# Wider rows for the modulation matrix, and an earlier silu, in a two-block kernel

## The chip, the cores and the metric

The kernel runs as one program on one core of one Trainium2 chip. The metric is the device time of one execution in microseconds (us); three executions of the kernel before took 1585.89, 1587.98 and 1588.04 us, and their median, 1587.98 us, is the time before. One more execution was recorded by the hardware profiler; it took 1586.62 us.

## The reference

Two transformer blocks follow each other on 256 tokens of width 1024, all in float32. The first block has a mixer (`w_in`, a short convolution and a gated recurrence), cross attention to 256 memory rows, and a mixture of 16 experts. The second block has two layers with three attention branches each; every layer takes its norms through a modulation that depends on a condition vector `c` (for the tokens) or `c_ctx` (for 256 context rows):

```python
for l in range(DEPTH_2):
    ...
    shift, scale, gate = jnp.split(jax.nn.silu(c) @ w_ada[l] + b_ada[l], 3, axis=-1)
    shift_c, scale_c, gate_c = jnp.split(jax.nn.silu(c_ctx) @ w_ada[l] + b_ada[l], 3, axis=-1)
    h = rms_norm_2(x, norm_g[l]) * (1.0 + scale[:, None]) + shift[:, None]
    hc = rms_norm_2(ctx, norm_g[l]) * (1.0 + scale_c) + shift_c
    ...
    x_new = x + gate[:, None] * merge_branches(o_na, o_mla, o_diff, z, gm, w_br[l], w_out[l])
```

`w_ada[l]` is 1024 x 3072, so 12 MB per layer are read to be multiplied by two vectors. None of this depends on the tokens: it can be computed at any time before the first norm of its layer.

## The kernel before, in words

**Order.** The kernel's instructions are written by a small planner inside the kernel file. Each part of the work is a generator ("fiber") with a priority and a clock of its own; `run` (L215) always takes the fiber that can start first by an estimate of each engine's time (`self.E`), and among equal ones that of the lowest priority number. `_pe` (L347) is its estimate for a matmul, `_later` (L248) moves a fiber's clock forward. The program is planned five times. Each pass fetches weights in the order in which the pass before used them, and the last pass repeats the order of the best of three. So a change of an estimate anywhere can move instructions everywhere.

**Weights.** All weights come in pieces ("units") of 512 KB, loaded by SyncE's queue in one fixed order (`_wdma`, L452), at most R units ahead (R is 5 at the start). A unit of most matrices is split by ScalarE and VectorE into two float32r parts, `wh` and `wl`, and used in three matmuls. A unit of `w_ada` is "plain": TensorE takes the float32 rows `w` as they landed.

**Modulation.** `ada(l)` (L1713) is a fiber of priority -6, ahead of everything. `silu_c` (L899) computes silu of both vectors and writes it 16 times over into `sil`, so that the stationary operand of a matmul has 32 columns. The four column groups of the array (32 columns each) then work on four pieces of `w_ada` at once and write four quarters of the partitions of one PSUM tile. A unit is two blocks of 128 rows by 512 columns of `w_ada` (runs of 2 KB in HBM); each block makes four matmuls of 128 moving columns, one for each column group. There are 24 units in a layer, in two PSUM tiles (4 and 2 column ranges of 512). When a tile is complete, ScalarE copies it out, TensorE transposes it, and VectorE adds the bias into `adacol`; from that `adaab` (the factors of the norm) is made.

Units of layer 1, and those of layer 0 but for the first `A0 = 2`, wait until the planner's TensorE clock is P1 = 4000 or P0 = 6000 ns further: they are strewn into the other work, one at a time.

**Start.** `setup` (L870) loads the tokens `X` on SyncE's queue, `cols` (all the short vectors, the two conditions among them) on ScalarE's, constants on GpSimd's. The fiber `tokens` starts at 5300 ns of the planner's clock (XT): a sum of squares on ScalarE and VectorE, a chain of tiny VectorE instructions for the inverse root, two scalings of X, 16 transposes on TensorE, the split of the transposed tokens into `hi` and `lo`, and the products with `w_in`. `silu_c` is started at 6800 ns by `context` (L2612): one ScalarE instruction and three of VectorE.

Of the kernel before, what the change touches and what calls it, by code (L numbers as in the profile page):

```python
# [14 lines left out]
OP = mybir.AluOpType  # L15
# [125 lines left out]
class Core:  # L141
# [14 lines left out]
    GPRIO, YPRIO = -1, 1.5  # L156
    MEMT, TOEP, CRIT = 40000, 20000, -4
    AH0, AH2 = 4, 1
    A0, P0, P1, AP0, AP1 = 2, 6000, 4000, -6, -6
    MFP = 0.5  # L160
    MEMP = 1
    GC, GW = 1, 7
# [1550 lines left out]
    def ada(self, l, *evs):  # L1713

        yield from self.wait(*evs)
        col = self.sb.tile([128, 24, 2], F32, name=f"adacol{l}", tag=f"adacol{l}", bufs=1)
        sil = self.sil.rearrange("p k r s -> p k (r s)")
        for g in ((0, 1, 2, 3), (4, 5)):
            ps = yield from self.palloc("pg")
            n = 128 * len(g)  # L1720
            for i, c in enumerate(g):
                for u in range(0, 8, 2):
                    if l or c * 4 + u // 2 >= self.A0:
                        self._later(self.E["pe"] + (self.P1 if l else self.P0))
                        yield
                    w = yield from self.wget("w_ada_2", (l,), u, u + 2, c * 512, c * 512 + 512, True)
                    for k in (u, u + 1):
                        for j in range(4):
                            self.mm(ps[32 * j:32 * j + 32, i * 128:i * 128 + 128], sil[:, k],
                                    w.raw[:, k - u, j * 128:j * 128 + 128], k == 0, k == 7, self.PAR[4])  # L1730
                        if k == u:
                            yield
                    self.wput(w)
                    yield
            r = yield from self.alloc("S", [128, 512])
            self.act(r[:, :n], ps[:, :n])
            self.free(ps)
            yield
            ps = yield from self.palloc("pa")
            for i in range(len(g)):  # L1740
                self.tr(ps[:, i * 128:i * 128 + 128], r[:, i * 128:i * 128 + 128])
            self.free(r)
            yield
            for i, c in enumerate(g):
                b = self.colv("b_ada", l * 24 + 4 * c, 4)
                pv = ps[:, i * 128:i * 128 + 128].rearrange("p (j r) -> p j r", j=4)
                self.tt(col[:, 4 * c:4 * c + 4], pv[:, :, 0:2], b[:, :, None].to_broadcast([128, 4, 2]), OP.add)
            self.free(ps)
            yield
        a = self.sb.tile([128, 2, 16], F32, name=f"adaab{l}", tag=f"adaab{l}", bufs=1)  # L1750
        for s in range(2):
            self.stt(a[:, s, 0:8], col[:, 8:16, s], 1.0, self.colv("norm_g", l * 8, 8), OP.add, OP.mult)
            self.cp(a[:, s, 8:16], col[:, 0:8, s])
        self.ada_ab[l], self.ada_g[l] = a, col
        self.set(self.ev_ada[l])
# [855 lines left out]

    def context(self):  # L2612
        norm = self.spawn(self.mem_norm(), prio=self.MEMP, t=self.MEMT)
        sil = self.spawn(self.silu_c(), prio=self.CRIT, t=6800.0, name="setup")
        self.ev_lb = self.spawn(self.lower(), prio=self.CRIT, t=self.LBT, name="setup")
        self.spawn(self.ada(0, sil), prio=self.AP0, name="ada")
        yield from self.mem_kv(norm)
        yield from self.ctx_hidden()
        yield from self.wait(self.ev_l0a)
        self.cur.prio = self.AP1  # L2620
        yield from self.ada(1)
# [114 lines left out]
```

## Time and profile before

| | before |
|---|---|
| median of 3 executions | 1587.98 us |
| their lowest and highest | 1585.89, 1588.04 us |
| profiled execution, its time | 1586.62 us |
| profiled execution, span from first to last instruction | 1584.8 us |
| TensorE busy | 1540.4 us, 97% |
| VectorE, ScalarE busy | 974.0 us, 749.4 us |
| moved by DMA | 305.15 MB, 48 loads of 512 KB of `w_ada` among them |

The span is what the views of the trace are measured in; the execution's own time has 1.8 us around it. PE is TensorE's matmuls, PEld its loading of stationary operands (which overlaps PE), DVE VectorE, ACT ScalarE, SP SyncE, whose queue issues the weight loads. A matmul of float32 on plain data shows as two records: the kernel has 384 of them in `ada`, the trace 768.

### The profile page before, as it was taken

Reading aid. Unit: us, or ns where it says so; the run is one execution under the profiler, and the core shown is the slowest. Engines: PE = TensorE matmul, PEld = TensorE weight load, DVE = VectorE, ACT = ScalarE, POOL = GpSimd, SP = SyncE. Lnnn points to the kernel's source line nnn. Section 1 sums busy time; section 2 is a strip of 40 time slices with the busy share of each in tenths; the row PEclk is TensorE's granted clock in tenths of the full one; section 3 lists DMA queues with packets and bytes.
Section 4 is the critical chain, followed back from the end, with each engine's and each line's share of the span. In section 5 each row is a group of like instructions: output and inputs, shape, how many; then the busy total and the mean of one; then the engine's idle time right before and its main releaser. Section 6 shows DMA issues by size and latency. Waiting matters only on the chain.

```text
span 1584.8 us, 25949 instructions
## 1 busy us (share of the span) xinstructions
PE 1540.4 (97%) x10202; PEld 1234.6 (78%) x10202; DVE 974.0 (61%) x1995; ACT 749.4 (47%) x1321; POOL 56.8 (4%) x91
## 2 busy tenths in 40 slices
PE   6999999999999999998999999999999999999898
PEld 6899897763554458886888777888888879989797
DVE  5877557722132257768765454754897766967755
ACT  5525345422322145747643345553464465645652
POOL 0000030000000001011000000000010200000000
PEclk9999999999999999999999999999999999999999
DMA  9766676589999996655324444443755425333341
GB/s 343 247 209 217 201 221 230 173 309 380 386 386 349 347 381 199 184 159 123 101 82 129 134 153 133 136 101 129 242 173 164 116 67 147 116 105 94 117 152 65
DMA packets 198939, 305.15 MB, mean 193 GB/s; under 512 B 10672, under 2 KB 97456, under 8 KB 198816
## 3 DMA queue, kind: packets, MB, share of 16 engines
q1 hardware_dynamic: 194384, 293.11, 56.3%
q0 software_dynamic: 3856, 9.64, 2.2%
q8 instruction: 81, 1.33, 0.3%
q10 hardware_dynamic: 576, 0.72, 0.2%
q14 instruction: 42, 0.34, 0.1%
HBM read 302.34 MB, written 2.90 MB: 193 GB/s over the span
## 4 chain that ended last, share of the span: by engine, by line
PE 60%; DVE 4%; ACT 1%; issue 1%; DVEq 0%; ACTq 0%
PE p L369 56%; PE p L374 4%; DVE t L392 1%; ACT t L382 1%; DVE wl L392 1%; DVE t L404 1%; DVE t L411 0%; ACT wh L382 0%; DVE t L413 0%; DVE X L392 0%; DVE p L392 0%; DVE t L397 0%; DVE t L399 0%; DVE t L406 0%; DVE t L420 0%
## 5 line engine op out<-in xcount | busy, mean ns | idle before, releaser
L369 PE MATMUL p<-t,wh 128*128 128x256 f32 (+1 forms) x2640 | 562.4, 309 | 0.0
L392 DVE TENSOR_TENSOR wl<-w,wh 128x1024 fp32r<-128x1024 f32 (+3 forms) x314 | 371.4, 1205 | 149.7 <-ACT wh L382 144.0
L369 PEld LDWEIGHTS p<-t,wh 128*128 128x128 f32 x2640 | 424.7, 190 | 32.5 <-issue 9.4
L369 PE MATMUL p<-wh,t 128*128 128x512 f32 (+1 forms) x1288 | 414.8, 394 | 2.3 <-DVE t L404 1.9
L369 PE MATMUL p<-t,wl 128*128 128x256 f32 (+1 forms) x1312 | 399.6, 305 | 2.2 <-DVE wl L392 2.2
L382 ACT ACTIVATE t<-p 128x512 f32<-128x512 f32 (+5 forms) x381 | 192.3, 528 | 411.3 <-PE p L369 316.8
L382 ACT ACTIVATE wh<-w 128x1024 fp32r<-128x1024 f32 (+3 forms) x314 | 316.8, 1042 | 58.5 <-PE p L369 23.4
L369 PEld LDWEIGHTS p<-wh,t 128*128 128x128 f32 x1288 | 242.8, 189 | 59.2 <-issue 6.8
L369 PEld LDWEIGHTS p<-t,wl 128*128 128x128 f32 x1312 | 249.8, 190 | 13.6 <-DVE wl L392 2.8
L369 PE MATMUL p<-wl,t 128*128 128x512 f32 (+1 forms) x644 | 251.1, 390 | 3.3 <-DVE wl L392 3.2
L369 PE MATMUL p<-t,t 128*64 128x128 f32 (+8 forms) x1824 | 222.4, 309 | 7.6 <-ACT t L382 6.2
L369 PEld LDWEIGHTS p<-t,t 128*64 128x64 f32 (+3 forms) x1824 | 177.3, 170 | 52.8 <-issue 24.9
L382 ACT ACTIVATE t<-p,t 128x512 f32<-128x512 f32 (+2 forms) x200 | 115.2, 597 | 126.6 <-PE p L369 84.0
L369 PE MATMUL p<-w,t 128*64 128x512 f32 x768 | 174.8, 598 | 0.0
L369 PEld LDWEIGHTS p<-wl,t 128*128 128x128 f32 x644 | 121.9, 189 | 27.1 <-DVE wl L392 5.1
L374 PE MATMUL p<-csts,t 128*128 128x128 f32 (+1 forms) x848 | 120.7, 278 | 12.8 <-ACT t L382 5.8
L369 PEld LDWEIGHTS p<-w,t 128*64 128x64 f32 x768 | 51.6, 136 | 95.6 <-issue 89.7
L374 PEld LDWEIGHTS p<-csts,t 128*128 128x128 f32 (+1 forms) x848 | 96.5, 140 | 34.5 <-ACT t L382 13.4
L392 DVE TENSOR_TENSOR t<-t,t 128x512 f32<-128x512 f32 (+9 forms) x226 | 106.4, 499 | 15.8 <-ACT t L382 13.0
L382 ACT ACTIVATE t<-p,cols 128x256 fp32r<-128x256 f32 (+4 forms) x91 | 51.3, 606 | 109.7 <-PE p L374 75.5
L411 DVE TENSOR_REDUCE t<-p 128x1 f32<-128x512 f32 (+1 forms) x124 | 84.7, 683 | 29.4 <-PE p L369 28.2
L404 DVE SCALAR_TENSOR_TENSOR t<-t,p 128x512 f32<-128x512 f32 x70 | 47.6, 683 | 78.7 <-PE p L369 39.8
(96 smaller groups left out, 694.0 us busy)
## 6 DMA issues: line engine op xcount, KB each, us to landing
w<-in_w_in_dram SPq DMA_DIRECT2D x206, 512.0 KB, 4.5
w<-in_w_gate_dram SPq DMA_DIRECT2D x64, 512.0 KB, 10.7
w<-in_w_up_dram SPq DMA_DIRECT2D x64, 512.0 KB, 10.6
w<-in_w_down_dram SPq DMA_DIRECT2D x64, 512.0 KB, 10.7
w<-in_w_ada_dram SPq DMA_DIRECT2D x48, 512.0 KB, 4.4
w<-in_w_out_dram SPq DMA_DIRECT2D x32, 512.0 KB, 4.3
w<-in_w_br_dram SPq DMA_DIRECT2D x28, 512.0 KB, 3.4
w<-in_w_kv_dram SPq DMA_DIRECT2D x16, 512.0 KB, 4.4
```

The lines of the kernel that those rows point to most:

```text
L369: self.nc.tensor.matmul(out, lhsT, rhs, start=start, stop=stop)
L374: self.nc.tensor.transpose(out, in_, self.ident[:k, :k])
L382: self.nc.scalar.activation(out, in_, func, bias=bias, scale=scale, **kw)
L392: self._e(eng, self._n(out), False, after).tensor_tensor(out, a, b, op=op)
L404: e.scalar_tensor_tensor(out, a, s, b, op0=op0, op1=op1)
L411: e.tensor_reduce(out, a, axis=AX, op=op, negate=True)
```

## The change

A unit of `w_ada` becomes one block of 128 rows by 1024 columns (runs of 4 KB), and each column group takes 256 of these columns in one matmul. A layer has three column ranges of 1024 instead of six of 512. For the first PSUM tile the two column ranges alternate inside the loop over the eight row blocks. The number of units, loads, bytes, copies out, transposes and bias additions stays; the number of matmuls is halved. The first *three* row blocks of the first column range are now free of the planner's spacing (A0 = 3); all units of the second and third range keep it. `silu_c` starts at 3500 ns of the planner's clock, ahead of the tokens' 5300.

```diff
-    A0, P0, P1, AP0, AP1 = 2, 6000, 4000, -6, -6
+    A0, P0, P1, AP0, AP1 = 3, 6000, 4000, -6, -6
...
-        for g in ((0, 1, 2, 3), (4, 5)):
+        for g in ((0, 1), (2,)):
             ps = yield from self.palloc("pg")
-            n = 128 * len(g)
-            for i, c in enumerate(g):
-                for u in range(0, 8, 2):
-                    if l or c * 4 + u // 2 >= self.A0:
+            n = 256 * len(g)
+            for k in range(8):
+                for i, c in enumerate(g):
+                    if l or c or k >= self.A0:
                         self._later(self.E["pe"] + (self.P1 if l else self.P0))
                         yield
-                    w = yield from self.wget("w_ada_2", (l,), u, u + 2, c * 512, c * 512 + 512, True)
-                    for k in (u, u + 1):
-                        for j in range(4):
-                            self.mm(ps[32 * j:32 * j + 32, i * 128:i * 128 + 128], sil[:, k],
-                                    w.raw[:, k - u, j * 128:j * 128 + 128], k == 0, k == 7, self.PAR[4])
-                        if k == u:
-                            yield
+                    w = yield from self.wget("w_ada_2", (l,), k, k + 1, c * 1024, c * 1024 + 1024, True)
+                    for j in range(4):
+                        self.mm(ps[32 * j:32 * j + 32, i * 256:i * 256 + 256], sil[:, k], w.raw[:, 0, j * 256:j * 256 + 256],
+                                k == 0 and i == 0, k == 7 and i == len(g) - 1, self.PAR[4])
                     self.wput(w)
                     yield
...
-            for i in range(len(g)):
+            for i in range(2 * len(g)):
                 self.tr(ps[:, i * 128:i * 128 + 128], r[:, i * 128:i * 128 + 128])
...
             for i, c in enumerate(g):
-                b = self.colv("b_ada", l * 24 + 4 * c, 4)
-                pv = ps[:, i * 128:i * 128 + 128].rearrange("p (j r) -> p j r", j=4)
-                self.tt(col[:, 4 * c:4 * c + 4], pv[:, :, 0:2], b[:, :, None].to_broadcast([128, 4, 2]), OP.add)
+                for h in range(2):
+                    b = self.colv("b_ada", l * 24 + 8 * c, 8)[:, h::2]
+                    m = 2 * i + h
+                    pv = ps[:, m * 128:m * 128 + 128].rearrange("p (j r) -> p j r", j=4)
+                    self.tt(col[:, 8 * c + h:8 * c + 8:2], pv[:, :, 0:2], b[:, :, None].to_broadcast([128, 4, 2]), OP.add)
...
-        sil = self.spawn(self.silu_c(), prio=self.CRIT, t=6800.0, name="setup")
+        sil = self.spawn(self.silu_c(), prio=self.CRIT, t=3500.0, name="setup")
```

## Rows read from the trace of the kernel before

**Rows 1.** The page: busy us (share of the span) and instructions by engine.
```profile
PE 1540.4 (97%) x10202; PEld 1234.6 (78%) x10202; DVE 974.0 (61%) x1995; ACT 749.4 (47%) x1321; POOL 56.8 (4%) x91
```

**Rows 2.** Windows, by stage: span, busy (instructions) of PE, PEld, DVE, ACT, POOL, clock, DMA.
```profile
60.00:205.00 145.00, 145.00 (x1179) 129.85 (x1178) 100.72 (x156) 57.52 (x77) 2.99 (x2) 1.00 0.62 206
...
870.00:1010.00 140.00, 139.02 (x1066) 109.64 (x1067) 77.74 (x217) 61.32 (x125) 0.00 (x0) 1.00 0.44 141
```

**Rows 3.** Waits of PE over the whole span: us in total, times, longest us.
```profile
PE p L369 <- DVE t L397: 11.1, 1, 11.1
...
PE p L374 <- DVE t L392: 4.2, 2, 3.2
...
PE p L369 <- DMA w<-in_w_ada_dram: 0.2, 1, 0.2
```

**Rows 4.** Timeline of PE around the unit at 23.32 us.
```profile
22.87 0.40 PE L369 MATMUL p<-t,wh 128*128 128x256 f32 x2
23.11 0.28 PE L369 MATMUL p<-t,wl 128*128 128x256 f32 x1
23.32 0.64 PE L369 MATMUL p<-w,sil 128*32 128x128 f32 x16
23.89 0.50 PE L369 MATMUL p<-t,wh 128*128 128x256 f32 x2
```

**Rows 5.** Windows inside that unit: span, PE busy (records begun), clock, DMA.
```profile
23.30:23.48 0.18, 0.16 (x8) 1.00 1.08 347
23.30:23.56 0.26, 0.24 (x8) 1.00 1.06 347
23.30:23.59 0.29, 0.27 (x12) 1.00 1.07 350
...
23.30:23.70 0.40, 0.38 (x16) 1.00 1.07 353
```

**Rows 6.** Window over plain matmuls of 512 columns, two column groups (64 wide).
```profile
328.30:335.70 7.40, 7.34 (x34) 1.00 0.52 179
```

**Rows 7.** Timeline of PE, start of the program.
```profile
11.11 1.08 PE L369 MATMUL p<-w,sil 128*32 128x128 f32 x16 [11.11 <-DVE t L397]
12.37 1.08 PE L369 MATMUL p<-w,sil 128*32 128x128 f32 x16 [0.17 <-DMA w<-in_w_ada_dram]
13.38 2.75 PE L374 MATMUL p<-csts,t 128*128 128x128 f32 x16
...
16.63 0.50 PE L369 MATMUL p<-t,wh 128*128 128x256 f32 x2
```

**Rows 8.** Timeline of ACT and DVE, start of the program.
```profile
6.25 1.06 ACT L382 ACTIVATE t<-X 128x1024 f32<-128x1024 f32 x1 [3.76 <-DMA X<-in_x_dram]
...
9.77 1.15 ACT L382 ACTIVATE t<-X,t 128x1024 f32<-128x1024 f32 x1 [2.26 <-DVE t L404]
13.85 1.06 ACT L382 ACTIVATE wh<-w 128x1024 fp32r<-128x1024 f32 x1 [2.93 <-DMA w<-in_w_in_dram]
...
10.07 0.29 DVE L416 COPY sil<-silc 128x256 f32<-128x256 f32 x1
10.28 0.75 DVE L397 TENSOR_SCALAR t<-X,t 128x1024 f32<-128x1024 f32 x1
```

**Rows 9.** DMA issues: the load of cols, KB and us from issue to landing.
```profile
cols<-in_cols_dram ACTq DMA_DIRECT2D x1, 80.5 KB, 3.4
```

**Rows 10.** Waits of PE in the first 60 us: us in total, times, longest us.
```profile
PE p L369 <- DVE wl L392: 0.7, 2, 0.5
```

**Rows 11.** Windows while X (4 KB rows), then mostly w_in (1 KB rows) lands; last column GB/s.
```profile
3.40:6.20 2.80, 0.00 (x0) 0.00 (x0) 1.00 1.05 425
17.50:23.50 6.00, 0.00 (x0) 0.00 (x0) 1.00 1.08 357
```

**Rows 12.** The tile adaab: made and used, duration ns, first and last start us.
```profile
L399 DVE TENSOR_SCALAR t<-p,adaab x16: 531/535/544, 263.5 to 1179.7; 128x256 f32<-128x256 f32 x16
L404 DVE SCALAR_TENSOR_TENSOR adaab<-adacol,cols x4: 157/161/164, 206.7 to 1012.1; 128x8 f32<-128x8 f32 x4
```

## The prediction

> **What bounds the kernel now.** I read the page's busy times first: PE is busy 1540.4 us of 1584.8, 97% [rows 1]. So TensorE bounds the kernel, and only two things can change the time: what an instruction occupies on TensorE, and where TensorE waits. Windows by stage came next, to see the stages that hold the units of `w_ada` (11 to 200 us and 875 to 1008 us). From 60 to 205 us PE has no idle time at all; from 870 to 1010 us it has 1 us in 140 [rows 2]. What a unit costs there is therefore paid in full, and what it saves is gained in full. The list of waits says the same from the other side: one wait of 11.1 us at the start, and after it nine groups, some 28 us in 30 pieces, none over 3.2 us; for a load of `w_ada`, the last group, PE waited once, 0.2 us [rows 3]. So neither the loads nor the rest of `ada` hold anything up; the start and the matmuls themselves are what is left to look at.
>
> **The units' matmuls.** The records of a unit overlap, so what counts is the distance of starts. In the unit at 23.32 us, the first record starts at 23.32 and the next other matmul at 23.89: 0.57 us [rows 4]. The windows inside it show how that is made: eight records have begun by 23.48 and no more by 23.56, twelve by 23.59, sixteen by 23.70 [rows 5]. So four column groups start together, in four rounds, the later ones 0.11 us apart (16 records in four rounds, the first at 23.32 and the last just before 23.70, so that the first gap is some 0.13), and a round of 128 columns takes as long as one group's columns take to stream. Is there a price per instruction in it that half as many would halve? The same kind of matmul with 512 columns on two column groups shows it: 34 records, 17 rounds, in 7.34 us, or 0.432 us a round [rows 6]. Four rounds of 128 columns at 0.109 are 0.436. Rounds of 128 and of 512 columns so take the same time per column, and two rounds of 256 will take about 0.43 too. What a unit costs beyond that, 0.57 - 0.43 = 0.14 us, lies before the second round and after the last (0.22 from the last round to the next matmul, against 0.11 within), where the array goes over between four groups and one; that happens once in a unit before and after. Ends: nothing, where it all belongs to the change-over, and 0.14 x 48 units = 6.7 us, where it all went; slower than now is excluded by the 512-column rounds. I take 0.01 us a unit, 0.5 us, near the lower end, because the windows place the 0.14 us at the two edges of a unit [rows 5].
>
> The Trainium skill says otherwise (TensorEngine Tiling (Array Packing), Instruction Overhead): each matmul carries some 60 cycles, and one should not shorten a dimension that is already small. By that rule, 8 records fewer in a unit, at an estimated 25 ns each by that page, would give 0.2 us x 48 = 9.6 us one after another, or a quarter of it, 2.4 us, with four groups side by side; the trace's 0.109 us for 128 columns beside 0.432 for 512 leaves no room for 25 ns a round.
>
> **Runs of units.** Going into a unit costs 23.32 - 23.11 = 0.21 us where the matmuls before it were 0.12 apart, and coming out 0.11 more than a round: 0.2 us for each run of units that stand together [rows 4, 5]. Before, the first two stand together [rows 7]. After, a unit of the free first three of column range 0 can only follow a spaced one of range 1, so that I expect two pairs (second and third unit, fourth and fifth) and one run fewer: 0.2 us less, between 0 and 0.4.
>
> **The start.** The move of the silu takes one ScalarE instruction from behind the sum of squares and three of VectorE (the last from 10.07 to 10.36 us) from between the inverse root and the scaling of X [rows 8]. No DMA goes with it: `cols` is loaded in any case, at the head of ScalarE's queue, and lands 3.4 us after its issue, about 4 us into the span [rows 9], while X arrives at 6.25 [rows 8]. The new place adds one wait: ScalarE waits for `cols` with the sum of squares queued behind it, covered by 2 us; if that cover failed, all that follows would be late by the difference. The scaling of X on VectorE can end some 0.5 us sooner, but ScalarE's half ends at 10.92 in either case, so X is ready 0.1 us earlier than the 11.03 of now. What is late next is the first unit's load: PE starts at 11.11 with two units [rows 7], and the second waited 0.17 us for its load, so that the first landed little before 11.
>
> Those two units occupy PE from 11.11 to 13.38, 2.27 us, at a slower pace than later ones (1.08 against 0.64 us a unit); the 16 transposes stand behind them [rows 7]. After the change the second unit is spaced 6 us on the planner's clock, so only one stands before the transposes, which start near 12.1, 1.25 us sooner. That is no gain yet: the unit is done later, at some 0.66 us (0.57 and the way in), and a transpose that runs earlier runs at the slower pace. PE had no gap from 13.38 to the first product at 16.63, so most of the 1.25 us is work moved, not time saved; what can go are the 0.17 us and the 0.7 us that PE waits for `wl` in the first 60 us [rows 10]. The first `w_in` unit stands one place earlier in SyncE's queue, and ScalarE, which waited for it until 13.85 [rows 8], gets it one load's time sooner, about 1.4 us (next part), so the transposed tokens need not wait behind that split. Ends: a gain of 2.3 us (both units out of the way, nothing paid back) and a loss of 1.4 us (the first product still waits until 16.6, and both displaced units are paid later). I take a gain of 0.7 us.
>
> **Loads and the rest.** While 4 KB rows of X land, the rate is 425 GB/s, while mostly 1 KB rows of `w_in` land, 357 [rows 11]: 512 KB in 1.23 or 1.47 us, so rows of 4 KB save at most 0.24 us a load. Nobody waits for these loads after the first, so I count nothing; with that cover gone it would be 48 x 0.24 = 11.5 us of queue time, most of it where the DMA engines are half idle. The bias additions keep their number, and `adaab` has 57 us from its making (206.7) to its use (263.5) in layer 0, and more in layer 1 [rows 12]: nothing. Halved estimates and one spacing fewer in layer 0 shift the planner's clock, so all later instructions are ordered anew; that has no sign that I can read, and I give it the size of the longest inner wait, 3.2 us, either way [rows 3].
>
> **Sum.** 0.5 + 0.2 + 0.7 = 1.4 us faster. From the profiled execution's 1586.62 us that is 1585.2, from the median 1587.98 (1.36 us above it; the runs lie between 1585.89 and 1588.04) 1586.6. I take the middle, 1585.9 us. Against the median, 0.2% is 3.2 us, about what a measurement can tell from no change: faster is below 1584.8, slower above 1591.2.
>
> **Rivals**, from the middle of both bases, 1587.3 us.
> First, that half of the 0.14 us a unit does belong to the number of instructions: 0.07 x 48 = 3.4 us, with the other 0.9 together 4.3 us, 1583.0. For it speaks that the first round's gap is 0.13, not 0.11; against it, that the equal pace of 128 and 512 columns leaves the price at the edges.
> Second, slower: pairs of `w_ada` units stand in SyncE's queue ahead of `w_in` units in the first 25 us, where loads land one after another at full rate and PE already waits for `wl` twice [rows 10]. Each overtaken load is late by some 1.4 us (between 1.23 and 1.47, above); four of them make 5.6, less 0.7 for the matmuls, 1592.2. It decides from three overtaken loads on. Against it speaks that a planner's load is five units ahead.
> Third, that the start gives nothing, since it is the same work on a busy engine: 0.7 us, 1586.6.
>
> **How the numbers follow.** My forecast 0.48, with its own range 1583.5 to 1588.5; of it 0.14 lies below 1584.8. First rival 0.22, all faster. Second 0.15, of which 0.12 is slower beyond the bound. Third 0.15, no change. Faster 0.36, the same 0.52, slower 0.12. The range reaches to the first rival less the reordering's 3.2 us, 1579.8, and to near the second's price, 1591.5, which leaves out half of that rival.
>
> **What would show it.** A unit's 8 records in two rounds 0.21 to 0.22 us apart, 0.56 to 0.57 us from first record to next matmul, and the tile `sil` with 384 records, would show the main step right; 0.50 or less would show the first rival. One unit before the transposes, these at 12.0 to 12.2 us and the first product near 15.5, with silu's instructions before 6.25 us, would show the start. Waits on `wl` in the first 60 us of several microseconds, against 0.7 now, would show the second. The prediction is wrong where PE's busy time or its inner 28 us of waits change by more than 3 us for another reason.

## The result and the profile after

The change made the kernel slower: 1598.39 us (median of 4 runs, 1595.89 to 1600.34) beside 1588.01 us (4 runs, 1585.89 to 1588.51). The ratio is 1.0061, between 1.0045 and 1.0078. The forecast was 1585.9 us in a range of 1579.8 to 1591.5, and the time lies above that range. Run again beside other kernels, the same program took 1597.88 us, ratio 1.0061 (1.0047 to 1.0074).

The page of the kernel after (the profiled execution took 1595.89 us) has TensorE's busy time and count in its first lines:

```profile
span 1594.1 us, 25181 instructions
...
PE 1543.0 (97%) x9818; PEld 1226.4 (77%) x9818; DVE 973.5 (61%) x1995; ACT 749.4 (47%) x1321; POOL 56.6 (4%) x91
```

Against [rows 1], 384 matmuls are gone, and the busy time has risen by 2.6 us; the span is 9.3 us longer (1594.1 against 1584.8). So nothing was won on the matmuls, and some 7 us are idle time. The list of TensorE's waits after (total us, times, longest us) says where to look; but for the first, the groups shown are new or larger than before:

```profile
PE p L369 <- DVE t L397: 10.8, 1, 10.8
...
PE p L369 <- DVE wl L392: 6.4, 6, 1.9
...
PE p L374 <- DVE t L392: 5.2, 5, 3.2
PE p L374 <- DVE t L397: 3.9, 5, 1.3
PE p L369 <- PEq L1644: 2.8, 1, 2.8
...
PE p L369 <- ACT wh L382: 1.3, 1, 1.3
```

Before, the waits for `wl` were 5.4 us, those for `t` of L392 and L397 on the transposes 4.2 and 2.8, and there was none for `wh`. One more line of that list answers to the jump (L1644):

```profile
PE p L369 <- PEq L1644: 0.3, 1, 0.3
```

**The units.** TensorE's timeline after, around one unit in the steady stretch, answers to [rows 4]:

```profile
32.22 0.28 PE L369 MATMUL p<-t,wl 128*128 128x256 f32 x1
32.43 0.64 PE L369 MATMUL p<-w,sil 128*32 128x256 f32 x8
33.00 0.50 PE L369 MATMUL p<-t,wh 128*128 128x256 f32 x2
```

From the first record to the next other matmul it is 33.00 - 32.43 = 0.57 us, as before, with 8 records in place of 16. The way in is 0.21 us (32.43 - 32.22), also as before.

**The start.** TensorE's first records after, beside [rows 7]:

```profile
10.78 1.08 PE L369 MATMUL p<-w,sil 128*32 128x256 f32 x8 [10.78 <-DVE t L397]
11.79 3.05 PE L374 MATMUL p<-csts,t 128*128 128x128 f32 x16
14.77 1.07 PE L369 MATMUL p<-w,sil 128*32 128x256 f32 x16
17.10 0.50 PE L369 MATMUL p<-t,wh 128*128 128x256 f32 x2 [1.26 <-ACT wh L382]
18.36 0.39 PE L369 MATMUL p<-t,wl 128*128 128x256 f32 x1 [0.76 <-DVE wl L392]
...
23.84 0.38 PE L369 MATMUL p<-t,wl 128*128 128x256 f32 x1 [0.95 <-DVE wl L392]
```

One unit stands ahead of the transposes, and these begin 1.6 us sooner. But the first product comes at 17.10, not 16.63, after a wait of 1.26 us for ScalarE's split of the first `w_in` unit, and two waits for `wl` follow. SyncE's timeline (start, us, of load issues) says why. Before:

```profile
1.24 0.99 SPq L458 DMA_DIRECT2D w<-in_w_ada_dram  x2
2.27 0.80 SPq L458 DMA_DIRECT2D w<-in_w_in_dram  x1
3.12 0.58 SPq L458 DMA_DIRECT2D w<-in_w_ada_dram  x1
3.74 2.25 SPq L458 DMA_DIRECT2D w<-in_w_in_dram  x1
6.03 2.15 SPq L458 DMA_DIRECT2D w<-in_w_ada_dram  x1
```

After:

```profile
1.25 1.85 SPq L458 DMA_DIRECT2D w<-in_w_ada_dram  x3
3.13 0.74 SPq L458 DMA_DIRECT2D w<-in_w_in_dram  x1
3.92 1.07 SPq L458 DMA_DIRECT2D w<-in_w_ada_dram  x2
5.04 8.95 SPq L458 DMA_DIRECT2D w<-in_w_in_dram  x3
```

Three units of `w_ada` stand ahead of the first of `w_in` where two stood, and five ahead of the second where three stood. In the first 25 us SyncE issues 8 loads of `w_ada` and 10 of `w_in`, against 6 and 11.

**Where the time went.** Matching the same matmul in the two traces gives the lag of one behind the other at a point of the program; the differences of the lag are what each stretch cost. "Again" is the second profile of the change; the next four columns belong to experiments below. What the rows leave to the last one lies behind 1358 us.

```
us against before         change  again  e_rows  e_afterpad  e_sameplan  e_pad
start to 206 us            +1.19  +1.04   +0.22       +1.31       -0.50  -0.64
206 to 328                 +0.57  +2.32   +0.74       +0.78       +2.77  +0.97
328 to 506                 -0.28  -0.39   -0.38       +0.48       -0.38  -0.39
506 to 601 (the branch)    +3.62  +3.87   +3.80       +0.99       +3.78  +0.85
601 to 783                 -0.78  +1.04   +0.98       +1.15       -0.01  -0.05
783 to 918                 +1.46  -0.13   -0.14       -0.14       +1.45  -0.14
918 to 1066                +1.98  +1.94   +1.99       +2.01       -0.15  -0.15
1066 to 1358               +1.52  +1.59   +1.50       -0.10       +0.14  +0.02
at the end                 +9.26 +11.26   +9.18       +6.50       +7.07  +0.48
```

The first row ends at 206 us because there all these kernels have done the 24 units of layer 0. At 37 us the change lags by 2.2 us, but it has done six units where before has done five, so part of that is work moved forward and not time lost.

**The branch behind the experts.** TensorE's timeline after, where the program jumps over the overflow body (L1644):

```profile
522.77 4.46 PE L369 MATMUL p<-w,t 128*64 128x512 f32 x20
530.02 0.76 PE L369 MATMUL p<-wh,t 128*128 128x512 f32 x1 [2.79 <-PEq L1644]
530.58 0.63 PE L369 MATMUL p<-wl,t 128*128 128x512 f32 x1
```

and before:

```profile
526.09 0.47 PE L369 MATMUL p<-wh,t 128*128 128x512 f32 x1 [0.34 <-PEq L1644]
526.39 0.40 PE L369 MATMUL p<-wl,t 128*128 128x512 f32 x1
```

The same jump holds TensorE for 2.79 us in place of 0.34. What follows it runs slower: its first matmul takes 0.76 us, not 0.47. The window behind it after (span, busy of PE, PEld, DVE, ACT, POOL, granted clock, DMA share, GB/s):

```profile
530.00:534.20 4.20, 4.18 (x12) 3.16 (x12) 0.00 (x0) 0.00 (x0) 0.00 (x0) 0.66 0.42 139
```

The granted clock averages 0.66 there: for most of it TensorE ran at the lower of its two levels, 1.2 GHz. No code of this place was touched by the change.

**The new order.** Two waits of the kernel after have no counterpart in before. The first is in layer 1:

```profile
983.74 0.64 PE L369 MATMUL p<-w,sil 128*32 128x256 f32 x8
985.67 1.13 PE L374 MATMUL p<-csts,t 128*128 128x128 f32 x8 [1.29 <-DVE t L397]
...
1294.73 0.66 PE L374 MATMUL p<-csts,t 128*128 128x128 f32 x4 [0.74 <-ACT t L382]
1296.79 0.66 PE L374 MATMUL p<-csts,t 128*128 128x128 f32 x4 [0.38 <-ACT t L382]
1298.13 3.35 PE L369 MATMUL p<-t,t 64*128 64x256 f32 x39 [0.37 <-ACT t L382]
```

A unit stands there in front of transposes, and when it is done VectorE still has to make their input; the three rows at 1295 us replace one of 0.24 us. In the second place stands no unit of `w_ada` at all. Only the order of the instructions, which the planner made anew, is different.

### The profile page after: what moved, and what is told of

Same layout as the page of the kernel before. It is cut to its first block, busy times and chain, and to the rows that moved or that the text cites. A ratio compares the mean times of both kernels' runs of the same rounds, so it can differ in the third digit from the quotient of the medians.

```text
span 1594.1 us, 25181 instructions
## 1 busy us (share of the span) xinstructions
PE 1543.0 (97%) x9818; PEld 1226.4 (77%) x9818; DVE 973.5 (61%) x1995; ACT 749.4 (47%) x1321; POOL 56.6 (4%) x91
## 4 chain that ended last, share of the span: by engine, by line
PE 59%; DVE 5%; ACT 2%; issue 1%; DVEq 0%; ACTq 0%
PE p L369 55%; PE p L374 4%; DVE t L392 2%; ACT t L382 1%; DVE wl L392 1%; DVE t L404 1%; ACT wh L382 0%; DVE t L411 0%; DVE t L413 0%; DVE X L392 0%; DVE p L392 0%; DVE t L399 0%; DVE t L397 0%; DVE t L406 0%; DVE t L420 0%
## 5 line engine op out<-in xcount | busy, mean ns | idle before, releaser
L392 DVE TENSOR_TENSOR wl<-w,wh 128x1024 fp32r<-128x1024 f32 (+3 forms) x314 | 370.9, 1203 | 147.0 <-ACT wh L382 141.4
L392 DVE TENSOR_TENSOR t<-t,t 128x512 f32<-128x512 f32 (+9 forms) x226 | 105.9, 496 | 19.5 <-ACT t L382 16.7
L404 DVE SCALAR_TENSOR_TENSOR t<-t,p 128x512 f32<-128x512 f32 x70 | 47.5, 683 | 80.5 <-ACT t L382 41.9
```

Source lines behind the costliest of these rows:

```text
L392: self._e(eng, self._n(out), False, after).tensor_tensor(out, a, b, op=op)
L404: e.scalar_tensor_tensor(out, a, s, b, op0=op0, op1=op1)
```

## The experiments

All times are medians; the ratio is to the kernel before on the same chip, run between them. It took 1587.93 us beside e_sameplan, e_rows, e_silu and e_free2, 1588.54 beside e_pad, e_padwr, e_beforewr and e_afterpad, and 1587.34 beside the rest.

**e_sameplan: the wide units alone.** Loads and matmuls as in the change, but the planner is told what it was told before: two matmuls of 128 columns for each of 256, the break inside a unit, the first two units free, the silu in its old place. So every other instruction keeps before's order.

```diff
-                    if l or c or k >= self.A0:
+                    if l or c == 2 or k * len(g) + i >= 2:
...
-                        self.mm(ps[32 * j:32 * j + 32, i * 256:i * 256 + 256], ...
+                        for _ in range(2):
+                            self._pe(4 * 128, 128, self.PAR[4], 2 * self.PEX)
+                        self.nc.tensor.matmul(ps[32 * j:32 * j + 32, i * 256:i * 256 + 256], ...
+                        if j == 1:
+                            yield
-        sil = self.spawn(self.silu_c(), prio=self.CRIT, t=3500.0, name="setup")
+        sil = self.spawn(self.silu_c(), prio=self.CRIT, t=6800.0, name="setup")
```

> Rows of 1024 columns alone, with the spacing rule, the silu and the planner's estimates of the kernel before, so that every engine has the order of instructions of before and only the 48 units differ. Theory 1 (the loss is the order at the start, a longer wait at the branch behind the experts and new places in the order, not the wide units): the start as before (first product near 16.6 us, 0.7 us of waits for wl in the first 60 us), a unit 0.57 us, time 1588 to 1591 us, of which up to 2.5 us is the branch if its wait hangs on the length of TensorE's instruction stream. Rival (wide rows or matmuls of 256 columns cost something by themselves): 1595 to 1599 us.

Measured: 1593.22 us, ratio 1.0028 (1.0017 to 1.0039). A unit of its timeline:

```profile
32.78 0.64 PE L1730 MATMUL p<-w,sil 128*32 128x256 f32 x8
33.35 0.51 PE L369 MATMUL p<-t,wh 128*128 128x256 f32 x2
```

The time is above the range of theory 1 and below that of the rival. A unit takes 0.57 us again. Its row of the tile `adaab`, beside [rows 12], shows the first layer's `ada` done at 206.2 us in place of 206.7:

```profile
L404 DVE SCALAR_TENSOR_TENSOR adaab<-adacol,cols x4: 154/156/157, 206.2 to 1019.1; 128x8 f32<-128x8 f32 x4
```

Not all of that is the units. Of the 0.50 us, 0.38 are there at 25 us, after four units, and a second profile of before is 0.21 us ahead of the first at both points without a wide unit. From 25 to 206 us, over 20 units, e_sameplan gains 0.12 us, and e_pad, which has the same units, 0.12 as well: some 0.006 us a unit, or by this estimate 0.3 us in all 48. So the wide units save a little less than the forecast gave them, and cost nothing. The kernel is slower nonetheless, and the table puts its loss in three other places: the branch (3.8 us), 2.8 us between 206 and 249 us, which are dealt with below, and 1.5 us at 890 us, where the clock falls.

**e_rows: the units as in the change, silu in its old place.** The planner counts the units as the change does; the first two are free.

```diff
-                    if l or c or k >= self.A0:
+                    if l or c == 2 or k * len(g) + i >= 2:
...
-        sil = self.spawn(self.silu_c(), prio=self.CRIT, t=3500.0, name="setup")
+        sil = self.spawn(self.silu_c(), prio=self.CRIT, t=6800.0, name="setup")
```

> Rows of 1024 columns with the changed kernel's own estimates, but the silu at 6800 ns and only the first two units free of spacing, as before. Theory 1: two units stand ahead of the first w_in load, as before, so the start loses nothing; branch wait as in e_sameplan; the rest is order alone: 1587 to 1592 us. Rival: as the change, 1595 to 1599 us.

Measured: 1595.39 us, ratio 1.0045 (1.0033 to 1.0057), outside the range of theory 1. Its start came as expected: SyncE's order of loads is that of before, TensorE waits for no `w_in` load in the first 60 us, and the lag at 206 us is 0.2 us, against 1.2 in the change. The waits at 985 and 1295 us are there with the same prices as in the change (table), and in e_sameplan they are not: they come from how the units are counted, which is all that lies between the two kernels beside the break inside a unit.

**e_silu: before, with the silu early and nothing else.**

```diff
-        sil = self.spawn(self.silu_c(), prio=self.CRIT, t=6800.0, name="setup")
+        sil = self.spawn(self.silu_c(), prio=self.CRIT, t=3500.0, name="setup")
```

> The kernel before with the silu at 3500 ns alone (units of 512 columns). Its queue has three units of w_ada ahead of the first w_in load instead of two. Theory 1: first product later than 16.6 us by up to 1.4 us, TensorE's waits before 25 us 1 to 2 us longer, branch wait 0.3 us as before, time 1589 to 1591 us. Rival (the early silu is harmless or good): 1586 to 1588 us.

Measured: 1596.21 us, ratio 1.0051 (1.0038 to 1.0064), a miss in size. This line alone moves SyncE's list to three units of `w_ada` ahead of the first of `w_in` and four ahead of the second. TensorE's first product in its timeline:

```profile
19.41 0.50 PE L369 MATMUL p<-t,wh 128*128 128x256 f32 x2 [1.87 <-ACT wh L382]
```

That is 2.8 us later than in [rows 7], and the lag is 5.4 us at 37 us, with five units done as in before, and 5.2 at 328. Some 1.4 us of it are not a wait: from 20.8 us on the granted clock is 0.5 for 3.4 us, and five times a group of three matmuls takes 0.64 us where it takes 0.36 at the full clock. Its branch waits 0.18 us. So the early silu is what spoils the start, for the most part through the loads, and it does so without the wide units.

**e_free2: the change, with the first two units free.**

```diff
-                    if l or c or k >= self.A0:
+                    if l or c == 2 or k * len(g) + i >= 2:
```

> The change with only the first two units free of spacing (no pairs), silu at 3500 ns. Three units ahead of the first w_in load, one fewer than the change ahead of the second. Theory 1: start 1 to 1.5 us behind before instead of 2.1, branch as in e_sameplan, 1590 to 1594 us. Rival (the pairs are the loss): 1587 to 1589 us.

Measured: 1600.67 us, ratio 1.0082 (1.0069 to 1.0095), a miss and the slowest of all. The start of its timeline:

```profile
11.99 1.11 PE L374 MATMUL p<-csts,t 128*128 128x128 f32 x4
13.04 1.08 PE L369 MATMUL p<-w,sil 128*32 128x256 f32 x8
14.05 2.26 PE L374 MATMUL p<-csts,t 128*128 128x128 f32 x12
18.50 0.50 PE L369 MATMUL p<-t,wh 128*128 128x256 f32 x2 [2.19 <-ACT wh L382]
```

The second free unit breaks into the transposes, as it does in e_silu, and the lag at 37 us is 5.1 us, part of it matmuls at the lower clock from 19 us on (0.63 us where 0.40 stands in the change). With one unit ahead of the transposes, as in the change, the clock did not fall there, and the early silu costs less than half of that. At the end the lag is 16.9 us; its five runs have a mean granted clock of 0.989, against 0.996 in those of before beside them, and where the rest lies was not traced.

**e_pad: e_sameplan with 48 more TensorE instructions ahead.** Twelve tiny matmuls on constants stand before the first unit, in time in which TensorE waits for the first scaled rows. They move the branch in TensorE's instruction stream and delay nothing by themselves.

```diff
+            for _ in range(12 if l == 0 and g[0] == 0 else 0):
+                self.nc.tensor.matmul(ps[0:32, 0:16], self.csts[:, 0:32], self.csts[:, 0:16], start=True, stop=True)
```

> e_sameplan with 12 tiny matmuls (32x16, on constants, overwritten later) put ahead of the first unit, while TensorE is idle; nothing else is moved. They only push the branch behind the experts 48 instructions further in TensorE's stream. Theory 1 (the wait at the branch, 2.74 us in e_sameplan and 0.34 before, hangs on where the branch lies in the stream of instructions that TensorE loads in pieces of 16 KB): the wait falls below 0.5 us and the time by 2.4 to 4 us, to 1589 to 1591 us. Rival (it comes from the wide loads or the experts' traffic): the wait stays 2.7 us, 1593 us.

Measured: 1589.49 us, ratio 1.0007 (0.9998 to 1.0016), against 1.0028 (1.0017 to 1.0039) without them. Behind the branch:

```profile
526.03 0.47 PE L369 MATMUL p<-wh,t 128*128 128x512 f32 x1 [0.34 <-PEq L1644]
526.33 0.40 PE L369 MATMUL p<-wl,t 128*128 128x512 f32 x1
```

The wait is back at 0.34 us. The ratios also hold what the clock did elsewhere: the mean granted clock is 0.992 in the seven runs of e_sameplan, and 0.995 in the twelve of e_pad as in those of before beside them. Wide units with before's order and a branch in a good place are as fast as before, to within what can be told apart.

**e_afterpad: the change with the same twelve matmuls.**

> The changed kernel with the same 12 tiny matmuls. Theory 1: the branch wait falls from 2.79 us below 0.5, 1594 to 1596 us. Rival: no change, 1597 to 1599 us.

Measured: 1594.71 us, ratio 1.0044 (1.0029 to 1.0059). Its branch waits 0.34 us, and the stretch from 506 to 601 us costs 0.99 us in place of 3.62. The intervals of the ratio with and without the twelve overlap; it is the stretch that shows the effect. What is left, 6.5 us of lag, is the start and the new order.

**e_beforepad: before with 32 tiny matmuls.** The test from the other side: it brings before's branch to the position that it has in the change, modulo 256 instructions.

```diff
+            for _ in range(32 if l == 0 and g[0] == 0 else 0):
```

> The kernel before with 32 tiny matmuls (128 instructions) at the idle start, so that the branch lies 128 instructions further on in TensorE's stream: from instruction 6677 (21 behind a multiple of 256) to about 6805 (149 behind one), which is where it lies in the change and in e_sameplan. Theory 1: the branch wait rises from 0.34 to some 2.7 us, the time by 2.4 to 4 us: 1590.5 to 1592.5 us. Rival (the wait has to do with wide units): stays 0.3 us, 1587 to 1588.5 us.

Measured: 1592.02 us, ratio 1.0037 (1.0023 to 1.0051). Behind the branch:

```profile
529.38 0.50 PE L369 MATMUL p<-wh,t 128*128 128x512 f32 x1 [2.58 <-issue]
529.73 0.40 PE L369 MATMUL p<-wl,t 128*128 128x512 f32 x1
```

The wait appears in the kernel before too, with nothing of the change in it, so it is the place of the branch that counts and not the presence of tiny matmuls. Here the clock did not fall behind it, and the stretch from 506 to 601 us costs 2.1 us. Of the other 2.1 us of the profile's lag, 0.6 lie in the start and 1.0 at 750 us, where the clock stayed low twice as long (6.8 us).

**e_beforewr and e_padwr: two constants loaded early.** The loss of e_sameplan between 206 and 249 us lies behind two loads that ScalarE's queue issues at 233 us (`wr`, 80 KB, and `lrows`, 256 KB), for which ScalarE waits in order and TensorE behind it. It looked like a collision that the wide rows bring. The test loads both on GpSimd's queue at 41 us, in before and in e_pad, and gives up four small buffers elsewhere to make room.

```diff
-        wr = yield from self.alloc("S", [128, 8, 20])
-        nc.scalar.dma_start(wr, ins["wr"])
...
+            nc.gpsimd.dma_start(self.wr0, self.ins["wr"])
+            nc.gpsimd.dma_start(self.lr0, bass.AP(tensor=rw.tensor, offset=rw.offset, ap=[[0, 128], [1, 512]]))
```

> The kernel before with the same early load of the router's weights and lrows: the partner of e_padwr, with units of 512 columns. Theory 1: the waits of 1.16 and 2.10 us at 240 to 245 us go, 1584 to 1586 us. Rival (the waits are covered by another late result): 1587 to 1588 us.

> e_pad with the router's weights and the lrows constants loaded on GpSimd's queue at about 41 us instead of on ScalarE's at 233 us, so that ScalarE no longer holds TensorE up at 240 to 245 us. Theory 1 (wide rows alone are 0.5 us faster at 206 us; the rest of e_sameplan's loss is the landing of these two loads, the branch and the clock behind the stalls): 1583 to 1587 us, at most e_beforewr's time. Rival (wide rows cost by themselves): 3 us or more over e_beforewr.

Measured: e_beforewr 1584.08 us, ratio 0.9969 (0.9957 to 0.9981); e_padwr 1582.97 us, ratio 0.9962 (0.9949 to 0.9975). Both beat both kernels, and by the same, as far as the intervals tell. So before has this wait as well, and by the medians it is worth 4.5 us there (1588.54 - 1584.08) and 6.5 in e_pad (1589.49 - 1582.97).

It is not what e_sameplan lost, though. TensorE's rows at this place, before and then in e_sameplan:

```profile
240.55 2.05 PE L369 MATMUL p<-t,t 128*128 128x256 f32 x8 [1.16 <-ACT t L382]
244.69 1.99 PE L369 MATMUL p<-t,t 128*128 128x256 f32 x8 [2.10 <-ACT t L382]
```

```profile
242.30 6.70 PE L369 MATMUL p<-t,t 128*128 128x256 f32 x16 [3.21 <-ACT t L382]
```

The waits are 3.26 and 3.21 us, but the same sixteen records take 4.04 us before and 6.70 in e_sameplan, where the granted clock is 0.54 from 241.5 to 249 us. Nor does the landing decide it. `wr` landed 6.6 us after its issue before and 8.8 in e_sameplan; in the second profile of before it took 8.6, the wait was 3.14, the sixteen took 3.79 with the clock up, and the stretch from 206 to 249 us cost 0.4 us less than in the first. The clock falls here in both profiles of the change, in e_sameplan and in e_rows, and in none of before, e_pad and e_afterpad, all with a wait of 2.6 to 4.2 us; why in the ones and not in the others stays open.

**e_start: the loads put in another order by hand.** To e_afterpad, a list of the first loads in the order ada, w_in, ada, ada, w_in, ada, ada, w_in.

```diff
+            j, k = [i for i, u in enumerate(order) if u[0] == "w_in"][:2]
+            order.insert(4, order.pop(k))
+            order.insert(1, order.pop(j))
```

> e_afterpad with one thing more: in the list of loads the first w_in unit stands right behind the first unit of w_ada, and the second behind the third (it was ada, ada, ada, w_in, ada, ada, w_in). Theory 1 (the start loses because w_in's loads stand behind those of w_ada, at about 1.4 us a load): the first product by 16.0 us instead of 17.1, the waits for wh and wl before 25 us (2.0 us in e_afterpad) below 0.8, and the time 1.5 to 2.5 us under e_afterpad's: ratio to before 1.002 to 1.0035. Rival (the start is bound elsewhere): as e_afterpad, ratio 1.0044.

Measured: 1597.74 us, ratio 1.0059 (1.0046 to 1.0073), a miss: slower than e_afterpad. Its timeline shows both halves:

```profile
15.02 0.50 PE L374 MATMUL p<-t,wh 128*128 128x256 f32 x2
...
25.93 0.39 PE L374 MATMUL p<-t,wl 128*128 128x256 f32 x1 [3.13 <-DVE wl L397]
```

The first product comes 2.1 us sooner, without a wait, and a later `w_in` unit is then 3.13 us late: moving two loads forward moved the wait to one behind them. By 328 us the lag is 6.6 us, part of it a 6.8 us wait at 248 us, where before waits 3.3. Whether some order of the first loads gives an early silu and no late `w_in` unit stays open.

**e_change2 and e_before2: both kernels once more.**

> The changed kernel once more, beside the others on one chip. Theory 1: the same branch wait of 2.8 us and the same waits before 25 us, at 985 and at 1295 us, ratio to before 1.0055 to 1.0065. Rival (the branch wait or the waits fall where the run lets them): other waits than in the first profile.

> The kernel before once more, for a second profile. Theory 1: branch wait 0.34 us, no wait at 985 us, router weights landed some 6.6 us after their issue. Rival: these vary from run to run by as much as they differ between the kernels.

Measured: the change 1597.88 us, ratio 1.0061 (1.0047 to 1.0074); before 1589.75 us in a single run. In the second profile of the change the branch waits 2.79 us again, the wait at 985 us is 1.29 again, and those at 1295 us are 0.74, 0.38 and 0.38. These are properties of the program. Before 25 us the waits for `wl` are 1.7 us again, but that for `wh` is 0.3 and not 1.26. In the second profile of before the branch waits 0.34 again, there is no wait at 985 us, and `wr` landed after 8.6 us and not 6.6.

Where the clock falls differs between two profiles of one kernel. Before has it at 298, 749 and 1274 us, and the second time also at 886 and 1483. The two are 3.1 us apart at the end: 1.5 lie at the fall at 886 us, and 1.6 between 384 and 388 us, where the second waits twice for a load of `w_up`. So +1.46 between 783 and 918 us in the first profile of the change, with a fall at 888 us, is no cost of the change, and neither is -0.10 in e_afterpad between 1066 and 1358 us a gain: it has the same waits at 1295 us, but no fall where before has one at 1274.

## Why the prediction was wrong, step by step

**The units: the mechanism right, the size a little high.** 8 records, 0.57 us from first record to next matmul, and some 0.006 us a unit saved in e_sameplan and e_pad, where 0.01 was forecast: 0.3 us in all for 0.5. The first rival, which gave half of 0.14 us to each instruction, falls: 0.50 us or less would have shown it. The Trainium skill (TensorEngine Tiling (Array Packing), Instruction Overhead) gives each matmul some 60 cycles. Read as a price on top, halving the count should have recovered it; this case's unit does not show it, with 0.57 us at either count.

**Runs of units:** too small to be seen behind the rest.

**The start: the step that failed in its argument.** The prediction said that the first `w_in` unit "stands one place earlier in SyncE's queue". It stood one place later, and the second one two places. The thought behind it was that one unit fewer ahead of the transposes is one load fewer ahead of `w_in`. But e_silu moves the loads with the silu alone, and in e_rows, with two units free and a late silu, they stand as before: it is the silu's time on the planner's clock that puts one more load of `w_ada` ahead of both; the second one ahead of the second `w_in` unit comes with the third free unit (e_silu and e_free2, with two free, have four there, the change five). The silu came in the forecast place and the transposes at 11.79, a little sooner than 12.0 to 12.2; the first product, forecast at 15.5, came at 17.10, and the waits for `w_in` before 25 us rose from 0.7 to 3.0 us (2.0 in the second profile). In place of a gain of 0.7 us the start costs some 1.2: 1.19, 1.04 and 1.31 us are left at 206 us in the three profiles with this start, and the gain of the first 24 units, 0.1, is in that. This is the second rival's mechanism, units of `w_ada` ahead of `w_in` in the first 25 us. Its place was right. That its price of 5.6 us is near what e_silu and e_free2 paid (5.4 and 5.1) is in part luck, because a fall of the clock is in both; the change paid about a quarter of it. One of the prediction's sums here is off as well: three overtaken loads give 1587.3 + 3 x 1.4 - 0.7 = 1590.8 us, below its bound of 1591.2, so that this rival decides from four on.

**Loads and the rest: the step that failed in size.** "Nobody waits for these loads after the first" is nearly true of `w_ada`, but the loads of `w_in` queued behind them are waited for, as just said. And the re-ordering, "no sign that I can read", stood in the sum as nothing, with 3.2 us either way. It costs about that by itself, and beside it stands a cost for which the prediction had no term. Its own sign of being wrong came true: the inner 28 us of waits became 35.
- The new order costs 2.0 us at 985 us and some 1.3 at 1295 us (0.74 + 0.38 + 0.37 - 0.24), 3.3 together. The first is in all six profiles of kernels that count wide units as the change does, the second in five of them (not in e_free2), and neither is in e_sameplan or e_pad, which have before's order.
- The shorter instruction stream moves the branch. 24 units of 8 matmuls and 8 weight loads fewer are 384 instructions, and the branch, which was free at its old place, costs 2.4 us more of wait. Its stretch costs 2.1 us with the clock up and 3.6 to 3.9 with the clock down behind the wait, and 0.5 to 1.0 in e_before2, e_pad and e_afterpad, where the wait is 0.34.

With 1.2 for the start, 3.3 for the order and some 3 for the branch, 7.5 us of the 10.4 have a place. By the ratios, a pair of kernels gives 3.3 us for the branch (e_sameplan 1.0028, e_pad 1.0007), in which the clock's falls elsewhere are contained, and another 5.9 us for start and order together (e_pad 1.0007, e_afterpad 1.0044), 9.2 in all. The rest, 2.9 us, is no more than the 3.1 by which two profiles of before differ; part of it is the fall of the clock at 243 us, and it was not traced further. The expected gain of the units was there, and it was a few tenths of a microsecond; three side effects of the edit, none of them at the units, stand against it.

## What to carry over

Before counting what an edit saves on a saturated engine, list what else it shifts: the order of a shared load queue, every planner's estimate, and the length of the instruction stream ahead of a taken branch. A branch that costs nothing in one build may cost microseconds in the next, and a few idle-time instructions ahead of it tell quickly whether a small loss is only that. Take a second profile of the kernel before, too: one fall of the clock that is absent in it looks like a cost of the change.

## What the runs showed of the hardware

**The price of a taken branch depends on where it stands.** The branch itself (its own duration in ns, then its start in us), in the kernel after:

```profile
L1644 PEldq COMPARE_BRANCH  x1: 6312/6312/6312, 523.4 to 523.4; - x1
```

Its own duration does not tell the price: in before it is 353 ns, with a wait of 0.34 us behind it, and in e_sameplan 353 ns as well, with 2.74.

Instructions arrive by a DMA queue of their own. Its row on the page (packets, MB) for before and then for after:

```profile
q8 instruction: 81, 1.33, 0.3%
```

```profile
q8 instruction: 78, 1.28, 0.3%
```

1.33 MB in 81 packets is 16.4 KB each. The traces have 20,641 instructions of TensorE before and 19,867 after, so 255 to a packet in both: the queue carries TensorE's stream, and 384 matmuls and as many weight loads fewer are three pieces of 256. Near the branch, before fetches pieces at 511.1 and 526.0 us, the change at 498.9, 527.1 and 530.4. In the five profiles with a wait of over 2 us, the last piece ahead of the branch was fetched some 24 us before it, and the next one within 0.3 us of the start of the wait; in all others a piece came 1 to 15 us before the branch. The number of TensorE instructions ahead of the branch, what is left of it over a multiple of 256 (modulo), and the wait behind it:

```
kernel                  instructions  modulo 256  wait, us
before, e_before2               6677          21      0.34
e_beforewr                      6677          21      0.34
e_silu                          6725          69      0.18
e_beforepad                     6804         148      2.58
e_sameplan                      6293         149      2.74
change, e_change2               6294         150      2.79
e_rows                          6295         151      2.70
e_pad, e_padwr                  6340         196      0.34
e_afterpad, e_start             6341         197      0.34
e_free2                         6343         199      0.18
```

The Trainium skill (Runtime: NRT & Kernel Launch, Instruction fetch mechanics) says that instructions come in blocks of 16 KiB, 256 instructions each, read ahead in sequence, and that a taken branch to a target outside the blocks held must wait for a fetch. The runs agree with the blocks and with a fetch at the wait; that TensorE waits for this very fetch is read from the times, no view names it. They add the price, some 2.4 us, and that it is paid at some positions only. Between 69 and 148, and between 151 and 196, no run says where it begins and ends.

**A small load can be slow.** The 80 KB of `wr` landed 6.6 to 9.6 us after issue in the profiles in which ScalarE's queue issues it between 232 and 239 us, with no difference in the program between the two of before (6.6 and 8.6) or the two of the change (8.0 and 9.6); the 80.5 KB of `cols` at the start took 3.4 [rows 9]. How long TensorE then waits behind it does not follow from the landing alone: 3.3 and 3.1 us in the two profiles of before.
